# Moving the small parameter loads and the rows of x from SyncE's DMA queue to ScalarE's

## The chip, the cores and the metric

The kernel runs on one core of a Trainium2 chip. The metric is device time in microseconds (us) of one execution. A core has five engines that work in parallel, each on its own instructions in a fixed order: TensorE (PE in the profile; PEld is its weight load), VectorE (DVE), ScalarE (ACT), GpSimd (POOL) and SyncE (SP). Transfers are carried out by 16 DMA engines; an instruction on some engine's queue issues them. Here SP issues nearly all of them and does nothing else.

## What is computed

Two layers of a decoder trunk on x of 256 rows by 2048 columns, in float32. Each layer has a mixer and a feed-forward part; both are modulated by six vectors that a large matrix `w_ada` makes of one condition vector c. The opening of the kernel computes the first two of these vectors (`sh_m`, `sc_m`) for layer 0, the modulated input u and its projection:

```python
cond = silu(c)                                        # 1 x 2048
for l in range(2):
    mod = (cond @ w_ada[l] + b_ada[l]).reshape(B, 6, 1, 2048)    # w_ada[l]: 2048 x 12288
    sh_m, sc_m, gt_m, sh_f, sc_f, gt_f = [mod[:, i] for i in range(6)]
    u = x * (1 + sc_m) + sh_m
    proj = u @ w_in[l]                                # 2048 x 4896
    y_attn = sliding_window_attention(q, k, v of proj, attn_sinks[l], cos, sin)
    y_rwkv = rwkv7_group(rest of proj, rwkv_mu[l], w0, w2, a0, a2, g2, k_k, k_a, r_k, gn_w, gn_b, ...)
    mix = concatenate([y_attn, y_rwkv]) @ w_out[l]
    x = layer_norm(alpha * x + gt_m * mix, ln1_w[l], ln1_b[l])
    u = x * (1 + sc_f) + sh_f
    gate, up = split(u @ w_gate_up[l])
    x = layer_norm(alpha * x + gt_f * ((silu(gate) * up) @ w_down[l]), ln2_w[l], ln2_b[l])
```

## The kernel before

Each float32 operand of a matrix product is split into a rounded part `hi` and a rest `lo`, so that a product takes three TensorE matmuls: hi·hi, hi·lo and lo·hi. For a weight tile `raw` ScalarE makes `hi` by a cast (L380) and VectorE makes `lo` by a subtraction (L381); `steps` (L367 and following) does both and issues the load of `raw` (L372).

**The opening.** `parts` (from L1285) cuts the 16 blocks of 128 columns of x (k-tiles) into five groups of 4, 4, 2, 4 and 2. For each group it takes these steps:

- `ada_first` streams the columns of `w_ada` that belong to the group, in 16 tiles `ast` of 512 KB (L301). They lie in 8 buffers. VectorE multiplies each by its scalars of `cond` and adds it to the accumulator `aacc` (L304 for the first, L306 for the others).
- `ada_sums` transposes the accumulator on TensorE in blocks of 128 (tile `mb`, L277), ScalarE sums the rows of each block (L281), eight sums in a group of four k-tiles, and VectorE adds the bias `b_ada` and stores `mods` (L284), one instruction for every four sums.
- x comes in as the tile `xt` (L1300), two buffers in all. `make_u` transposes it (L354), ScalarE makes `uf` and its rounded form `u` from it with the `mods` (L358, L360), and VectorE makes the rest (L361).
- `tstream` multiplies `u` with the columns of `w_in` that the RWKV part needs first (L414 to L416).

Between the steps of the first group the generator `setup` is run for layer 0, and between those of the third group for layer 1. It loads all parameters that belong to a channel into a tile `prow` of 128 rows: `b_ada`, `ln1_w` and `ln1_b` (L175), ten others (L185), the last columns of `rwkv_mu` (L189) and, for layer 1, `rwkv_v0` (L193). Further it loads the attention sinks into `nsink` (L194). TensorE transposes `prow`, VectorE copies it to `par` (L200) and derives a few vectors `der` from it. `prow` has one buffer; the tile of layer 1 takes it when the one of layer 0 has been transposed. At the end of `parts`, `rope` loads the positions and makes tables of angles, and two DRAM tiles `tinv` are filled with zeros (L1313).

While this goes on, `ada_steps` streams the rest of `w_ada` in tiles of 128 x 1024 (L253, multiplied on L255 and L257); these go on far into the layer.

**What sets the order.** The program is written as generators, and a scheduler that estimates durations decides at build time in which order each engine gets its instructions. So an edit to one line can move instructions elsewhere. What a DMA must wait for is set then too. Eight semaphores, DMAHW0 to DMAHW7, are handed to the transfers in turn, in scheduled order, whatever the queue. A transfer is issued only when the one that had its semaphore before has landed, when its buffer is free and when its data exist; until then the issuing engine's queue stands, and with it all that follows on that engine.

The name `dma` in the code is `nc.sync.dma_start`, the queue of SP.

Of the kernel before, what the change touches and what calls it, by code (L numbers as in the profile page):

```python
# [19 lines left out]
P = 128  # L20
# [47 lines left out]
def hybrid_trunk_kernel(  # L68
# [7 lines left out]
    nc = tc.nc  # L76
    V, S, G, PE = nc.vector, nc.scalar, nc.gpsimd, nc.tensor
    dma = nc.sync.dma_start

    const = ctx.enter_context(tc.tile_pool(name="const", bufs=1))  # L80
    lhsp = ctx.enter_context(tc.tile_pool(name="lhsp", bufs=17))
# [69 lines left out]
    nsink = [const.tile([P, 16], F32, name=f"nsink{l}") for l in range(L)]  # L151
# [14 lines left out]
    def drv(l, nm, i, n=1):  # L166
        return der[l][:, DO[nm] + i:DO[nm] + i + n]

    def setup(sp, l):

        prow = sp.tile([P, 2, P], F32, tag="prow", bufs=1, name=f"prow{l}")
        G.memset(prow, 0.0)
        r = 0
        for nm, src, n in (("b_ada", b_ada[l], 96), ("ln1_w", ln1_w[l], 16), ("ln1_b", ln1_b[l], 16)):
            dma(prow[r:r + n, 0, :], src.rearrange("(r q) -> r q", q=P))  # L175
            PC[nm] = r
            r += n
            yield
        r = 0
        lst = [("ln2_w", ln2_w[l], 16), ("ln2_b", ln2_b[l], 16), ("w0", rwkv_w0[l], 8),  # L180
               ("a0", rwkv_a0[l], 8), ("k_k", rwkv_k_k[l], 8), ("k_a", rwkv_k_a[l], 8),
               ("r_k", rwkv_r_k[l].rearrange("h d -> (h d)"), 8), ("gn_w", rwkv_gn_w[l], 8),
               ("gn_b", rwkv_gn_b[l], 8), ("mu", rwkv_mu[l, 0:26 * P], 26)]
        for nm, src, n in lst:
            dma(prow[r:r + n, 1, :], src.rearrange("(r q) -> r q", q=P))  # L185
            PC[nm] = P + r
            r += n
            yield
        dma(prow[r:r + 1, 1, 0:32], rwkv_mu[l:l + 1, 26 * P:26 * P + 32])  # L189
        r += 1  # L190
        PC["v0"] = P + r
        if l > 0:
            dma(prow[r:r + 8, 1, :], rwkv_v0[l - 1].rearrange("(r q) -> r q", q=P))  # L193
        dma(nsink[l], attn_sinks[l:l + 1, :].to_broadcast([P, 16]))  # L194
        V.tensor_scalar_mul(nsink[l], nsink[l], -1.0)
        yield
        pt = bank()
        for i in range(2):
            PE.transpose(pt[:, i * P:(i + 1) * P], prow[:, i, :], ident)
        V.tensor_copy(par[l].rearrange("p a b -> p (a b)"), pt[:, 0:2 * P])  # L200
        V.tensor_scalar(drv(l, "omu", 0, 27), prm(l, "mu", 0, 27), -1.0, 1.0, ALU.mult, ALU.add)
        V.tensor_scalar_mul(drv(l, "w0h", 0, 8), prm(l, "w0", 0, 8), 0.5)
        V.tensor_scalar_mul(drv(l, "a0h", 0, 8), prm(l, "a0", 0, 8), 0.5)
        V.tensor_scalar_mul(drv(l, "kah", 0, 8), prm(l, "k_a", 0, 8), 0.5)
        V.tensor_scalar(drv(l, "okah", 0, 8), prm(l, "k_a", 0, 8), -0.5, 1.0, ALU.mult, ALU.add)
        V.tensor_scalar_mul(drv(l, "kkh", 0, 8), prm(l, "k_k", 0, 8), -0.5)
        V.tensor_scalar_mul(drv(l, "v0h", 0, 8), prm(l, "v0", 0, 8), 0.5)
# [1078 lines left out]
    with tc.tile_pool(name="pro", bufs=1) as pp:  # L1286
        xv = x[0].rearrange("(t p) d -> p t d", p=P)

        def parts():
            k0 = 0  # L1290
            for n in PARTS:
                o, w = k0 * P, n * P
                xt = pp.tile([P, 2, 512], F32, tag="xt", name="xt", bufs=2)[:, :, 0:w]
                side = setup(pp, 0) if k0 == 0 else setup(pp, 1) if k0 == 8 else iter(())
                rows = ada_first(pp, o, w)
                for j in range(512 // w, KT + 1, 512 // w):
                    next(rows)
                    next(side, None)
                    if j == 8:
                        dma(xt, xv[:, :, o:o + w])  # L1300
                for _ in side:
                    pass
                for _ in rows:
# [48 lines left out]
```

## Time and profile before

| quantity | value |
|---|---|
| time, median of 3 runs | 2694.9 us |
| lowest and highest of them | 2692.5 and 2695.86 us |
| time of the profiled execution | 2694.28 us |
| its span in the trace | 2692.6 us |
| TensorE busy | 2501.1 us, 93% of the span |
| VectorE, ScalarE, GpSimd busy | 1841.0, 1188.3 and 135.0 us |
| chain that ended last: TensorE, DMA, VectorE | 68%, 8%, 6% |
| moved by DMA | 637.49 MB, 237 GB/s on average |

The profile is of one execution. An engine is busy while it carries out an instruction; waiting and issuing DMAs don't count. The chain is followed back from the last instruction, at each step to what released it. In a timeline the bracket behind a row gives how long the engine had been idle before it, and what ended that wait; a row with x6 stands for six instructions in a row, and its duration is that of all of them.

### The profile page before, as it was taken

The numbers are of one execution on the slowest core, as the hardware profiler recorded it, in microseconds if no ns is written. First come the engines' busy times: TensorE is split into PE (matmuls) and PEld (weight loads), VectorE is DVE, ScalarE is ACT, GpSimd is POOL, SyncE is SP. The second block draws the span as 40 slices with busy tenths as digits, with TensorE's granted clock in tenths as the row PEclk, the third lists the DMA queues.
The fourth block names the chain that finished last, engine by engine and source line by source line (L and its number), as shares of the span: only waits on it lengthen the run. The fifth ranks groups of instructions, "written<-read, shape, count | busy, mean of one in ns | idle before, by whom it ended". The sixth has DMA issues, their size and how long they took to land.

```text
span 2692.6 us, 41752 instructions
## 1 busy us (share of the span) xinstructions
PE 2501.1 (93%) x15325; PEld 2093.1 (78%) x15325; DVE 1841.0 (68%) x2469; ACT 1188.3 (44%) x2029; POOL 135.0 (5%) x355
## 2 busy tenths in 40 slices
PE   3788998788999999999999999979899999999997
PEld 2687886567888888888889877867688888888887
DVE  6866767979877777777788677555764545545456
ACT  2364452435444444444445544534444444344442
POOL 1002112000000000000000022110000000000000
PEclk9789998899999999999999999989999999999999
DMA  9968668688998888889878586424756656666654
GB/s 315 381 188 253 198 191 238 180 317 296 353 330 309 297 303 312 293 295 308 308 263 304 174 259 188 117 72 144 253 172 188 190 186 196 195 189 189 193 188 149
DMA packets 351999, 637.49 MB, mean 237 GB/s; under 512 B 75894, under 2 KB 142898, under 8 KB 350258
## 3 DMA queue, kind: packets, MB, share of 16 engines
q1 hardware_dynamic: 351794, 634.82, 71.6%
q8 instruction: 120, 1.97, 0.3%
q14 instruction: 85, 0.70, 0.1%
HBM read 622.08 MB, written 12.62 MB: 236 GB/s over the span
## 4 chain that ended last, share of the span: by engine, by line
PE 68%; DMA 8%; DVE 6%; ACT 2%; issue 1%; POOL 1%; SPq 0%; DVEq 0%; POOLq 0%; ACTq 0%
PE acc L403 19%; PE acc L402 19%; PE acc L405 19%; DMA ast<-in_w_ada_dram 3%; DVE aacc L257 2%; PE acc L414 2%; PE acc L415 2%; PE acc L416 2%; DVE lo L381 1%; DMA raw<-in_w_gate_up_dram 1%; PE mb L1225 1%; DMA raw<-in_w_out_dram 1%; DMA yf<-yd 1%; PE mb L277 1%; ACT pr L947 0%
## 5 line engine op out<-in xcount | busy, mean ns | idle before, releaser
L380 ACT CAST hi<-raw 128x1024 fp32r<-128x1024 f32 (+2 forms) x728 | 758.5, 1044 | 1110.8 <-PE acc L405 833.1
L381 DVE TENSOR_TENSOR lo<-raw,hi 128x1024 fp32r<-128x1024 f32 (+2 forms) x728 | 880.2, 1212 | 519.8 <-PE acc L403 347.1
L403 PE MATMUL acc<-lo,u 128*128 128x512 f32 x1568 | 513.4, 395 | 11.9 <-DVE lo L381 11.8
L405 PE MATMUL acc<-hi,u 128*128 128x512 f32 x1568 | 505.8, 391 | 0.0
L257 DVE SCALAR_TENSOR_TENSOR aacc<-ast,cond,aacc 128x1024 f32<-128x1024 f32 x300 | 384.1, 1280 | 127.8 <-DMA ast<-in_w_ada_dram 126.6
L402 PE MATMUL acc<-hi,u 128*128 128x512 f32 x1568 | 457.2, 393 | 0.9 <-ACT u L360 0.5
L403 PEld LDWEIGHTS acc<-lo,u 128*128 128x128 f32 x1568 | 293.8, 189 | 76.4 <-DVE lo L381 16.2
L402 PEld LDWEIGHTS acc<-hi,u 128*128 128x128 f32 x1568 | 294.9, 188 | 63.4 <-ACT sg L1218 0.9
L405 PEld LDWEIGHTS acc<-hi,u 128*128 128x128 f32 x1568 | 295.2, 188 | 61.8 <-issue 0.5
L403 PE MATMUL acc<-lo,ht 128*128 128x512 f32 (+1 forms) x720 | 243.6, 377 | 3.0 <-DVE lo L381 2.9
L405 PE MATMUL acc<-hi,ht 128*128 128x512 f32 (+1 forms) x720 | 242.2, 375 | 0.0
L414 PE MATMUL acc<-u,hi 128*128 128x256 f32 x720 | 206.1, 293 | 14.0 <-ACT hi L380 14.0
L402 PE MATMUL acc<-hi,ht 128*128 128x512 f32 (+1 forms) x720 | 217.0, 376 | 0.0
L415 PE MATMUL acc<-u,hi 128*128 128x256 f32 x720 | 204.5, 291 | 0.0
L416 PE MATMUL acc<-u,lo 128*128 128x256 f32 x720 | 193.1, 294 | 7.1 <-DVE lo L381 7.1
L403 PEld LDWEIGHTS acc<-lo,ht 128*128 128x128 f32 x720 | 135.0, 188 | 29.3 <-DVE lo L381 5.6
L414 PEld LDWEIGHTS acc<-u,hi 128*128 128x128 f32 x720 | 141.9, 197 | 19.3 <-ACT hi L380 14.9
L405 PEld LDWEIGHTS acc<-hi,ht 128*128 128x128 f32 x720 | 135.6, 188 | 24.2
L402 PEld LDWEIGHTS acc<-hi,ht 128*128 128x128 f32 x720 | 134.8, 188 | 24.4
L415 PEld LDWEIGHTS acc<-u,hi 128*128 128x128 f32 x720 | 141.7, 197 | 2.6 <-issue 1.6
L416 PEld LDWEIGHTS acc<-u,lo 128*128 128x128 f32 x720 | 133.8, 197 | 11.6 <-DVE lo L381 9.0
L1067 POOL TENSOR_TENSOR brs<-brs,mhalf 128x1 f32<-128x1 f32 x8 | 7.6, 955 | 1698.7 <-DVE brs L1066 772.1
(349 smaller groups left out, 2901.1 us busy)
## 6 DMA issues: line engine op xcount, KB each, us to landing
ast<-in_w_ada_dram SPq DMA_DIRECT2D x368, 512.0 KB
raw<-in_w_gate_up_dram SPq DMA_DIRECT2D x704, 256.0 KB
raw<-in_w_down_dram SPq DMA_DIRECT2D x176, 512.0 KB
raw<-in_w_in_dram SPq DMA_DIRECT2D x82, 512.0 KB
raw<-in_w_out_dram SPq DMA_DIRECT2D x64, 512.0 KB
raw<-in_w_in_dram SPq DMA_DIRECT2D x120, 256.0 KB
ast<-in_w_ada_dram SPq DMA_DIRECT2D x32, 256.0 KB
lnw<-in_ln_w_dram SPq DMA_DIRECT2D x4, 1024.0 KB
```

The lines of the kernel that those rows point to most:

```text
L257: ins = V.scalar_tensor_tensor(acc, t, cond[:, j:j + 1], acc, ALU.mult, ALU.add)
L277: PE.transpose(b[:, i * P:(i + 1) * P], blocks[q + i], ident)
L380: S.copy(h, fl)
L381: ins = V.tensor_tensor(r, fl, h.bitcast(F32), ALU.subtract)
L402: PE.matmul(bt, lhsT=xh, rhs=hi[:, c0:c0 + w], start=st, stop=False)
L403: PE.matmul(bt, lhsT=xh, rhs=lo[:, c0:c0 + w], start=False, stop=False)
L405: PE.matmul(banks[t][q][:, 0:w], lhsT=xl, rhs=hi[:, c0:c0 + w], start=False, stop=sp_)
L414: PE.matmul(bt, lhsT=hi[:, c0:c0 + w], rhs=xh, start=st and opens, stop=False)
L415: PE.matmul(bt, lhsT=hi[:, c0:c0 + w], rhs=xl, start=False, stop=False)
L416: PE.matmul(bt, lhsT=lo[:, c0:c0 + w], rhs=xh, start=False, stop=sp_ and closes)
L1067: G.tensor_tensor(rs[:, 0:1], rs[:, 0:1], mhalf[:, 0:1], ALU.pow)
L1225: PE.transpose(b[:, i * T + t * P:i * T + (t + 1) * P], hh[t][:, (2 * k2 + i) * P:(2 * k2 + i + 1) * P], ident)
```

## The change

A second name for issuing transfers is made, `side_dma`, which is the queue of ScalarE. The loads of `setup` (parameters into `prow`, and `nsink`) and the load of `xt` in `parts` use it. All others, the weights among them, remain on SP's queue. 36 issues move: 29 of parameters, 2 of `nsink`, 5 of `xt`. Lines after L77 have a number that is higher by one in the changed kernel.

```diff
@@ -76,6 +76,7 @@
     dma = nc.sync.dma_start
+    side_dma = nc.scalar.dma_start
@@ -172,7 +173,7 @@
         for nm, src, n in (("b_ada", b_ada[l], 96), ("ln1_w", ln1_w[l], 16), ("ln1_b", ln1_b[l], 16)):
-            dma(prow[r:r + n, 0, :], src.rearrange("(r q) -> r q", q=P))
+            side_dma(prow[r:r + n, 0, :], src.rearrange("(r q) -> r q", q=P))
@@ -182,16 +183,16 @@
         for nm, src, n in lst:
-            dma(prow[r:r + n, 1, :], src.rearrange("(r q) -> r q", q=P))
+            side_dma(prow[r:r + n, 1, :], src.rearrange("(r q) -> r q", q=P))
...
-        dma(prow[r:r + 1, 1, 0:32], rwkv_mu[l:l + 1, 26 * P:26 * P + 32])
+        side_dma(prow[r:r + 1, 1, 0:32], rwkv_mu[l:l + 1, 26 * P:26 * P + 32])
...
-            dma(prow[r:r + 8, 1, :], rwkv_v0[l - 1].rearrange("(r q) -> r q", q=P))
-        dma(nsink[l], attn_sinks[l:l + 1, :].to_broadcast([P, 16]))
+            side_dma(prow[r:r + 8, 1, :], rwkv_v0[l - 1].rearrange("(r q) -> r q", q=P))
+        side_dma(nsink[l], attn_sinks[l:l + 1, :].to_broadcast([P, 16]))
@@ -1297,7 +1298,7 @@
                     if j == 8:
-                        dma(xt, xv[:, :, o:o + w])
+                        side_dma(xt, xv[:, :, o:o + w])
```

The scheduler answers with other orders. Three places matter in what follows. In the rows, a line is followed by the operation and by what it writes and reads; the number behind a tile's name tells one tile from another, x6 is six in a row.

*SP, from the start of the program.* `ast` are weight tiles of `w_ada`, `prow_170` is the parameter tile of layer 0, `raw` are weight tiles of `w_in`. Before:

```order
L154 DMA crow<-in_c_dram 16x128
L301 DMA ast<-in_w_ada_dram 128x2x512 x6
L175 DMA prow_170<-in_b_ada_dram 96x128
L175 DMA prow_170<-in_ln_w_dram 16x128
L175 DMA prow_170<-in_ln_b_dram 16x128
L185 DMA prow_170<-in_ln_w_dram 16x128
L185 DMA prow_170<-in_ln_b_dram 16x128
L185 DMA prow_170<-in_rwkv_w_dram 8x128
L301 DMA ast<-in_w_ada_dram 128x2x512
L185 DMA prow_170<-in_rwkv_a_dram 8x128
L301 DMA ast<-in_w_ada_dram 128x2x512
L185 DMA prow_170<-in_rwkv_k_k_dram 8x128
```

And now:

```order
L155 DMA crow<-in_c_dram 16x128
L302 DMA ast<-in_w_ada_dram 128x2x512 x10
L373 DMA raw<-in_w_in_dram 128x2x256
L302 DMA ast<-in_w_ada_dram 128x2x512
L373 DMA raw<-in_w_in_dram 128x2x128
L302 DMA ast<-in_w_ada_dram 128x2x512
L373 DMA raw<-in_w_in_dram 128x2x256
L302 DMA ast<-in_w_ada_dram 128x2x512
L373 DMA raw<-in_w_in_dram 128x2x128
L302 DMA ast<-in_w_ada_dram 128x2x512 x2
L373 DMA raw<-in_w_in_dram 128x3x288
```

The parameters of layer 0 stood behind the sixth `ast` and between the later ones; now ten `ast` stand in a row, and then only weights follow.

*ScalarE, from the start of the program.* L281 are the row sums of the first group, L380 the casts of raw tiles, L358 and L360 make `u`. Before:

```order
L155 ACT_TABLE_LOAD
L155 ACTIVATE crow<-crow 16x128
L380 CAST hi<-raw 128x768 x2
L281 ACTIVATE mb,asum<-mb 128x128 x2
L380 CAST hi<-raw 128x864
L281 ACTIVATE mb,asum<-mb 128x128 x6
L358 ACTIVATE uf<-mb,mods_135 128x256
L360 ACTIVATE u<-mb,mods_135 128x256
L358 ACTIVATE uf<-mb,mods_135 128x256
```

And now, from the loads of layer 1's parameters (`prow_843`) on, with the semaphores that each waits for (those named DMAHW are the eight of the transfers; L282 is the old L281); ahead of these rows stand two loads of `xt`, two of `nsink`, the 14 of `prow_170`, the first casts and five loads of `prow_843`:

```order
L186 DMA prow_843<-in_rwkv_k_k_dram 8x128 [waits DMAHW0_49]
L186 DMA prow_843<-in_rwkv_k_a_dram 8x128 [waits DMAHW1_49]
L186 DMA prow_843<-in_rwkv_r_k_dram 8x128 [waits DMAHW2_49]
L186 DMA prow_843<-in_rwkv_gn_w_dram 8x128 [waits DMAHW4_49]
L186 DMA prow_843<-in_rwkv_gn_b_dram 8x128 [waits DMAHW5_49]
L282 ACTIVATE mb,asum<-mb 128x128 [waits DVE_49,PE_49]
L186 DMA prow_843<-in_rwkv_mu_dram 26x128 [waits DMAHW6_49]
L282 ACTIVATE mb,asum<-mb 128x128 [waits Activation_49]
L190 DMA prow_843<-in_rwkv_mu_dram 1x32 [waits DMAHW0_49]
L282 ACTIVATE mb,asum<-mb 128x128 [waits Activation_49]
L194 DMA prow_843<-in_rwkv_v_dram 8x128 [waits DMAHW1_49]
L282 ACTIVATE mb,asum<-mb 128x128 [waits Activation_49]
```

Loads for layer 1, which stood on SP and in the third group, now stand ahead of and between the first four row sums of the first group. `DMAHW6`, for which the load of `mu` waits (L186, 26x128), was last given to the seventh `ast` of the second group; `DMAHW0` in the first row was last given to a raw tile of the second group. The last two loads wait for loads of `prow_843` itself, those of the first two rows.

*VectorE, from the last multiply-add of the first group on.* `mods_135` are the modulation vectors of layer 0; L361, L381 and L306 are as described, and L224 to L241 belong to the tables of angles. Before:

```order
L306 SCALAR_TENSOR_TENSOR aacc<-ast,cond,aacc 128x1024
L381 TENSOR_TENSOR lo<-raw,hi 128x768 x2
L284 SCALAR_TENSOR_TENSOR mods_135<-asum,par_131 128x4
L304 TENSOR_SCALAR aacc<-ast,cond 128x1024
L284 SCALAR_TENSOR_TENSOR mods_135<-asum,par_131 128x4
L306 SCALAR_TENSOR_TENSOR aacc<-ast,cond,aacc 128x1024
L195 TENSOR_SCALAR nsink_138<-nsink_138 128x16
L221 CAST posf<-posi 128x2
L361 TENSOR_TENSOR u<-uf,u 128x256
```

And now (numbers higher by one), the rows around the two instructions that store `mods`:

```order
L242 TENSOR_SCALAR ang<-ang 128x64
L240 TENSOR_TENSOR rc<-rc,wrap 128x64
L307 SCALAR_TENSOR_TENSOR aacc<-ast,cond,aacc 128x1024
L242 TENSOR_SCALAR rc<-rc 128x64
L285 SCALAR_TENSOR_TENSOR mods_135<-asum,par_131 128x4
L256 TENSOR_SCALAR aacc<-ast,cond 128x1024
L285 SCALAR_TENSOR_TENSOR mods_135<-asum,par_131 128x4
L307 SCALAR_TENSOR_TENSOR aacc<-ast,cond,aacc 128x1024
L362 TENSOR_TENSOR u<-uf,u 128x256 x2
L307 SCALAR_TENSOR_TENSOR aacc<-ast,cond,aacc 128x1024 x2
L362 TENSOR_TENSOR u<-uf,u 128x256
```

The tables of angles, which came behind the `mods`, come ahead of them now; the two `mods` stand some sixteen rows further back, and 14 of the 16 multiplies of the second group stand behind the first of them.

## Rows read from the trace of the kernel before

**Rows 1.** The page: its first line and the busy time of each engine.
```profile
span 2692.6 us, 41752 instructions
...
PE 2501.1 (93%) x15325; PEld 2093.1 (78%) x15325; DVE 1841.0 (68%) x2469; ACT 1188.3 (44%) x2029; POOL 135.0 (5%) x355
```

**Rows 2.** Stretches: us, busy PE, PEld, DVE, ACT, POOL (count), PEclk, DMA share, GB/s.
```profile
0.00:20.00 20.00, 0.70 (x2) 0.36 (x2) 11.07 (x20) 1.59 (x2) 9.47 (x62) 1.00 0.81 262
20.00:40.00 20.00, 2.65 (x9) 1.61 (x9) 13.86 (x21) 5.32 (x19) 0.31 (x1) 1.00 1.03 358
40.00:60.00 20.00, 17.36 (x113) 16.19 (x114) 17.12 (x31) 6.80 (x13) 0.00 (x0) 1.00 0.93 305
...
80.00:140.00 60.00, 43.31 (x286) 40.10 (x286) 51.26 (x72) 23.46 (x63) 0.00 (x0) 0.83 1.07 380
...
0.00:2.50 2.50, 0.00 (x0) 0.00 (x0) 1.02 (x11) 1.44 (x2) 1.75 (x11) 1.00 0.12 13
```

**Rows 3.** Timeline of ACT from 32 us: start, us, engine, line, operation, idle before.
```profile
33.03 0.83 ACT L380 CAST hi<-raw 128x768 fp32r<-128x768 f32 x1 [30.38 <-DMA raw<-in_w_in_dram]
...
34.92 0.26 ACT L281 ACTIVATE mb<-mb 128x128 f32<-128x128 f32 x1
...
41.20 0.56 ACT L358 ACTIVATE uf<-mb,mods 128x256 f32<-128x256 f32 x1 [1.21 <-PE mb L354]
```

**Rows 4.** Timeline of DVE, the first group's multiplies.
```profile
5.48 0.89 DVE L304 TENSOR_SCALAR aacc<-ast,cond 128x1024 f32<-128x1024 f32 x1 [2.22 <-DMA ast<-in_w_ada_dram]
...
22.05 8.17 DVE L306 SCALAR_TENSOR_TENSOR aacc<-ast,cond,aacc 128x1024 f32<-128x1024 f32 x6 [2.85 <-DMA ast<-in_w_ada_dram]
```

**Rows 5.** Timeline of SP: its first weight tiles and parameters.
```profile
1.25 3.27 SPq L301 DMA_DIRECT2D ast<-in_w_ada_dram  x6
4.83 0.33 SPq L175 DMA_DIRECT2D prow<-in_b_ada_dram  x1
...
10.74 0.40 SPq L301 DMA_DIRECT2D ast<-in_w_ada_dram  x1
```

**Rows 6.** Waits of SP, 0 to 330 us: us in total, times, longest us.
```profile
SPq L185 <- DMA ast<-in_w_ada_dram: 8.3, 9, 1.5
```

**Rows 7.** Timeline of DVE, 37 to 80 us.
```profile
37.20 0.16 DVE L284 SCALAR_TENSOR_TENSOR mods<-asum,par 128x4 f32<-128x4 f32 x1 [1.33 <-ACT mb L281]
...
40.03 0.17 DVE L284 SCALAR_TENSOR_TENSOR mods<-asum,par 128x4 f32<-128x4 f32 x1 [2.01 <-ACT mb L281]
...
48.68 1.05 DVE L381 TENSOR_TENSOR lo<-raw,hi 128x864 fp32r<-128x864 f32 x1
...
49.75 0.42 DVE L361 TENSOR_TENSOR u<-uf,u 128x256 fp32r<-128x256 f32 x1
...
63.83 1.28 DVE L306 SCALAR_TENSOR_TENSOR aacc<-ast,cond,aacc 128x1024 f32<-128x1024 f32 x1 [2.19 <-DMA ast<-in_w_ada_dram]
...
71.30 1.22 DVE L381 TENSOR_TENSOR lo<-raw,hi 128x1024 fp32r<-128x1024 f32 x1 [1.03 <-ACT hi L380]
...
76.39 1.28 DVE L306 SCALAR_TENSOR_TENSOR aacc<-ast,cond,aacc 128x1024 f32<-128x1024 f32 x1
...
79.07 0.46 DVE L381 TENSOR_TENSOR lo<-raw,hi 128x288 fp32r<-128x288 f32 x1
```

**Rows 8.** Timeline of ACT, the end of the opening.
```profile
171.05 0.47 ACT L454 ACTIVATE xwa<-lb,der 128x256 f32<-128x256 f32 x1 [3.11 <-PE lb L416]
```

**Rows 9.** Waits of DVE, 80 to 140 us: us in total, times, longest us.
```profile
DVE mods L284 <- ACT mb L281: 2.6, 3, 1.1
...
DVE u L361 <- ACT u L360: 1.5, 3, 0.6
...
DVE lo L381 <- DMA ast<-in_w_ada_dram: 0.4, 1, 0.4
DVE aacc L306 <- DMA ast<-in_w_ada_dram: 0.4, 1, 0.4
```

**Rows 10.** The chain that ended last, 400 to 460 us: start, us, what.
```profile
412.53 5.83 DMA ast<-in_w_ada_dram
```

## The prediction

> **What bounds the kernel now.** I read the page first, then the opening of the kernel engine by engine, because that is where the edited lines run. TensorE is busy for 2501.1 of 2692.6 us [rows 1]; after the first 170 us the kernel is a stream of matmuls that hardly stops, and only a late start or a wait on the chain to TensorE can be won or lost there. The profiled execution took 2694.28 us, 0.6 us under the median of 2694.9, so that sums made in its trace stand as they are for the time.
>
> The opening is another matter. TensorE has done 0.70 us of work by 20 us and 2.65 us more by 40 us, while the DMA engines move 262, 358 and 305 GB/s in the first three stretches and 380 GB/s in 80 to 140 us [rows 2]. It is bound by the weights of w_ada. SyncE (its queue is SP) issues them as tiles `ast` of 512 KB; VectorE multiplies each into an accumulator (L306, 1.28 us a tile); after 16 tiles come transposes, eight row sums on ScalarE (L281) and the two `mods` (L284), and only then can ScalarE and VectorE make `u` (L358 to L361), which the first matmuls need. In the trace `u` starts at 41.20 [rows 3]. VectorE waits for `ast` more than once on the way, 2.85 us in one place [rows 4].
>
> Part of the low rate is SP's doing. SP issues six `ast` by 4.5 us, then a run of small parameter loads stands in the same queue, and its seventh `ast` goes out at 10.74 [rows 5]. Each such load also waits for the transfer that had its semaphore before it: nine waits of L185 cost SP 8.3 us [rows 6]. The eight DMA semaphores are handed round to the issues in the order of the program, whatever the queue, and an issue waits until the transfer eight turns earlier (on its semaphore) has landed.
>
> **What the change gives SP.** 36 issues leave SP's queue: 29 of parameters, 2 of `nsink`, 5 of x. One costs SP 0.33 us [rows 5] plus its wait. The most that this can give is the DMA rate of the steady stretch from the beginning: (380−262)·20 + (380−358)·20 + (380−305)·20 = 4300, divided by 380 is 11.3 us; the first 2.5 us carry 13 GB/s [rows 2] because nothing has landed yet, and no queue cures that, so 2.5·(380−13)/380 = 2.4 us come off: 8.9 us at most. The least is 0, if the later limits hide it.
>
> **What it adds to ScalarE.** In time of its own, 36 issues at 0.33 us are 12 us, in a stretch where ScalarE is busy for 1.59 + 5.32 + 6.80 of 60 us [rows 2]. Up to the first cast it waits 30.38 us for a raw tile [rows 3], and that idle time hides the first 18 issues and their own waits; without that cover they would cost 18·0.33 = 5.9 us. I count nothing for them.
>
> The waits of the next 15 are what I count. The order shown ahead puts the loads of *layer 1* (`prow_843`) in ScalarE's queue ahead of, and between, the first four row sums of the first group. A wait on one of their semaphores is a wait for what SP has put on it: that of `mu` is the seventh `ast` of the *second* group, and behind it are three of those four sums, all of the second four, and `u`. Before, nothing stood there, and the sums ran from 34.92, right behind the casts [rows 3].
>
> When does that tile land? Counting in SP's order what goes out up to it, in units of 512 KB: 16 + 7 `ast`, 2 tiles of x, 1344 KB of raw tiles of the first group, two of 260 KB (L1313), 2 `ast` of the mixer's own w_ada stream, 2 raw tiles of the second group and about 0.3 MB of small ones, together 33.3 units or 17.45 MB. The first unit lands at about 5.48, where the first multiply starts [rows 4]. At 380 GB/s one takes 0.5243/380 = 1.38 us, so the last is there at 5.48 + 32.3·1.38 = 50.0. That is an estimate, and it already contains the whole gain of the denser stream. `mods` came 37.20 − 34.92 = 2.3 us after the first sum and the second one 2.8 us later, at 40.03 [rows 3, 7]. So now: sums at 50, first `mods` at about 52.5, second at 55.5, `u` 1.2 us behind it (40.03 to 41.20) at 56.7 instead of 41.20: **15.5 us late**.
>
> Not all of that reaches the end, since VectorE has work in store. In the new order the first `mods` (L285 now) stands ahead of 14 of the second group's multiply-adds; VectorE runs dry near 38 and stands until 52.5. What is left for it up to the end of the second group is 14·1.28 + 4·0.42 (`u`) + 1.05 + 4·1.22 + 0.46 (`lo`) = 26.0 us [rows 7], and I put 3 us of waits on ScalarE and TensorE on top (from the single waits of 1.03 and 2.19 us among those rows). From 55.5 that ends at 84.5; before it ended at 76.39 + 1.28 = 77.7 [rows 7]. The late start has become 6.8 us.
>
> Is it made up by 171 us, where the opening ends with `xwa` on L454 [rows 8]? In 80 to 140 us VectorE is busy for 51.26 of 60 us [rows 2], and of its waits there those on w_ada's own tile before a multiply-add are 0.4 us, once; with a second such wait before a `lo`, 0.8 us may be regained [rows 9]. The larger ones, 2.6 us on row sums and 1.5 on `u`, belong to the chain itself [rows 9]. So **6 us** reach the end of the opening.
>
> Bounds of this term: it is 0 if nothing waits on TensorE or ScalarE and the semaphores come free at the earliest (26.0 us of work, sums released near 45 us, 5 us earlier: 50.5 + 26.0 is 76.5, before's 77.7). It is about +12 if the DMA engines keep to the mean of the first three stretches, 308 GB/s, for which the same 17.45 MB end at 5.48 + 32.3·1.70 = 60: sums 10 us later, of which VectorE's waits for `ast` then hide some half.
>
> On the rate a page speaks too. The trace of before has one queue with data, and shows the DMA engines at 380 GB/s from it when nothing holds it [rows 2]. The Trainium skill, "DMA: Bandwidth & Descriptors", section "Issuing engines are not separate DMA queues", says that transfers started by different engines run on the same 16 DMA engines and interleave, and that starting them on several saves only the sequencers' time to start them, usually a small one. By that rule the change would give back the issue time alone, which speaks against the gain and for the second rival below. The 8.3 us of waits in SP's row [rows 6] are more than issue time, so the row goes beyond the rule.
>
> **What moves beyond the opening.** The scheduler has reordered other stretches as well: VectorE's order is unchanged from about 200 to 400 us, then differs by some ten to forty places in the attention of layer 0 and around the mixer of layer 1, and in the last 690 us nothing moves. The multiset of instructions is the same. I know no sign for this. A single DMA wait on the chain costs 5.83 us there [rows 10]; one more or one fewer is my bound, ±5.8 us, and I take 0.
>
> **Sum.** 2694.3 + 6 + 0 = 2700 us. With the ends 0 and +12 and ±5.8 beside it: 2688 to 2712, the outer ends not both at once.
>
> **Rivals.**
> *Faster, by the denser stream.* All 8.9 us of the rate arrive: 2694.3 − 8.9 = 2685. For it: VectorE waits 2.85 us for an `ast` [rows 4] and SP does stand on semaphores of its own small loads [rows 6]. Against it: three of the first four sums wait for a tile of the second group. It decides at about 45 us: with the first group's sums released before that, VectorE isn't out of work long and the denser stream carries; after that the wait on ScalarE does.
> *No change.* SP's lateness was no more than its waits for transfers that the DMA engines were busy with anyway, and VectorE's store of work takes up the late sums: 2694. For it: VectorE works 42 of the first 60 us [rows 2] and needs 1.28 us per tile, hardly less than the 1.38 us that one takes to land.
> *The whole delay.* `u` is 15.5 us late and TensorE passes all of it on: 2710. Against it: VectorE, not TensorE, sets the pace of 80 to 140 us [rows 2].
>
> **Chances.** Forecast 0.55, faster rival 0.19, no change 0.19, the whole delay 0.07. A measurement of this kernel can tell about 0.2%, 5.4 us. Of the forecast's 0.55 I put 0.40 beyond +5.4 us and 0.15 within it. Faster by over 0.2%: 0.19. Within: 0.15 + 0.19 = 0.34. Slower: 0.40 + 0.07 = 0.47. The range runs from 2687, which takes in the forecast's lower end and nearly the faster rival, to 2711, which takes in the whole delay.
>
> **What would show it.** In the trace of after: six or more `ast` issued without a stop and over 340 GB/s in 0 to 20 us (the denser stream); ScalarE's waits for an `ast` or raw tile between its first sums, which end near 50; VectorE idle from about 38 to 52 ahead of the first `mods`; the last multiply-add of the second group near 84.5; `xwa` near 177 instead of 171. The prediction is wrong at its main step if the sums end before 45, wrong in what follows if they end at 50 and `xwa` is on time, and wrong in the reorder term if `xwa` is at 177 and the end isn't 6 us late.

## The result and the profile after

The changed kernel takes 2699.54 us (median of 18 runs, 2693.66 to 2706.76) against 2694.68 us of the kernel before (18 runs, 2687.27 to 2701.37): ratio 1.0021, 95% interval 1.0011 to 1.003. It is slower by about 5 us; the interval is clear of 1, and its middle lies at the 0.2% that I had set as a limit. The forecast was 2700. The profiled execution took 2702.37 us, 2.8 us above its median; that of before lay 0.4 us under its own, so the two traces differ by 8 us where the medians differ by 5.

The page of the changed kernel: its first line, the busy times and the two queues that now carry data (q10 is new).

```profile
span 2700.6 us, 41744 instructions
...
PE 2501.8 (93%) x15325; PEld 2093.4 (78%) x15325; DVE 1839.3 (68%) x2469; ACT 1188.1 (44%) x2029; POOL 128.6 (5%) x355
...
q1 hardware_dynamic: 349344, 632.46, 70.9%
q10 hardware_dynamic: 2450, 2.37, 0.3%
```

The engines are as busy as before [rows 1]: no work was added, it came later. By stretches, columns as in [rows 2]:

```profile
0.00:20.00 20.00, 0.70 (x2) 0.36 (x2) 10.76 (x22) 1.59 (x2) 7.08 (x62) 1.00 0.91 308
20.00:40.00 20.00, 1.56 (x5) 0.90 (x5) 15.22 (x26) 1.66 (x2) 0.31 (x1) 1.00 0.97 327
40.00:60.00 20.00, 2.23 (x8) 1.44 (x8) 4.70 (x13) 4.46 (x20) 0.00 (x0) 1.00 0.97 343
60.00:80.00 20.00, 18.13 (x132) 17.27 (x132) 17.38 (x18) 8.44 (x14) 0.00 (x0) 1.00 0.84 285
80.00:140.00 60.00, 45.84 (x311) 43.45 (x312) 55.11 (x73) 22.40 (x57) 0.00 (x0) 0.83 1.07 379
```

The stream is denser at first (308 GB/s instead of 262 in 0 to 20 us), as SP's timeline explains: ten tiles in a row, where six had stood [rows 5].

```profile
1.25 15.67 SPq L302 DMA_DIRECT2D ast<-in_w_ada_dram  x10
```

But in 40 to 60 us TensorE works for 2.23 us instead of 17.36 and VectorE for 4.70 instead of 17.12 [rows 2]. ScalarE's timeline shows why (ACTq rows are the DMAs that it issues; time and duration, then what it is):

```profile
29.48 0.83 ACT L381 CAST hi<-raw 128x768 fp32r<-128x768 f32 x1 [4.29 <-DMA raw<-in_w_in_dram]
40.28 0.32 ACTq L176 DMA_DIRECT2D prow<-in_b_ada_dram  x1
...
48.78 0.32 ACTq L186 DMA_DIRECT2D prow<-in_ln_b_dram  x1
49.14 0.91 ACT L381 CAST hi<-raw 128x864 fp32r<-128x864 f32 x1 [18.83 <-DMA prow<-in_ln_b_dram]
...
53.31 0.31 ACTq L186 DMA_DIRECT2D prow<-in_rwkv_gn_b_dram  x1
53.73 0.26 ACT L282 ACTIVATE mb<-mb 128x128 f32<-128x128 f32 x1 [3.67 <-DMA prow<-in_rwkv_k_k_dram]
...
54.10 0.31 ACTq L186 DMA_DIRECT2D prow<-in_rwkv_mu_dram  x1
54.47 0.26 ACT L282 ACTIVATE mb<-mb 128x128 f32<-128x128 f32 x1 [0.37 <-ACT mb L282]
...
59.67 0.56 ACT L359 ACTIVATE uf<-mb,mods 128x256 f32<-128x256 f32 x1 [1.21 <-PE mb L355]
```

Between the second cast at 29.48 and the third at 49.14 ScalarE does nothing but stand at loads of layer 1's parameters: the first of them goes out at 40.28, the fifth at 48.78, the twelfth at 53.31. The cast between them is put down to one of these loads, 18.83 us. The first row sum runs at 53.73 where it had run at 34.92 [rows 3], and `u` starts at 59.67 instead of 41.20. (Seven of these loads, not five, stand ahead of the rows of ScalarE's order shown with the change, so that twelve precede the first sum.)

What each load waited for, the semaphore updates in the trace tell. The first was released at 40.11 by a small load `w2a` that SP had issued at 33.20; the third, fourth and fifth at 44.56, 46.07 and 48.76 by tiles of w_ada that SP had issued at 37.04, 37.79 and 39.85; the eighth at 51.49 by a raw tile issued at 43.07. Apart from loads of their own group they all waited for SP's transfers, as the prediction has it. VectorE stands with ScalarE:

```profile
8.00 1.01 DVE L305 TENSOR_SCALAR aacc<-ast,cond 128x1024 f32<-128x1024 f32 x1 [3.69 <-DMA ast<-in_w_ada_dram]
...
55.67 0.16 DVE L285 SCALAR_TENSOR_TENSOR mods<-asum,par 128x4 f32<-128x4 f32 x1 [12.61 <-ACT mb L282]
...
58.50 0.16 DVE L285 SCALAR_TENSOR_TENSOR mods<-asum,par 128x4 f32<-128x4 f32 x1 [2.00 <-ACT mb L282]
...
85.04 1.28 DVE L307 SCALAR_TENSOR_TENSOR aacc<-ast,cond,aacc 128x1024 f32<-128x1024 f32 x1
```

Idle for 12.61 us ahead of the first `mods`; the second follows at 58.50. The second group's last multiply-add ends at 85.04 + 1.28 = 86.3, against 77.7 [rows 7].

VectorE's standing comes back to the weights: an `ast` needs a buffer that a multiply-add has freed. SP's waits for multiply-adds, 40 to 80 us (us in total, times, longest), before and in the changed kernel, and before's stretch of 60 to 80 us:

```profile
SPq L301 <- DVE aacc L306: 0.2, 1, 0.2
```
```profile
SPq L302 <- DVE aacc L307: 10.5, 9, 2.9
```
```profile
60.00:80.00 20.00, 10.07 (x69) 9.63 (x67) 14.34 (x14) 3.85 (x7) 0.00 (x0) 0.74 1.05 378
```

In 60 to 80 us the changed kernel moves 285 GB/s where before moved 378. By the rates of the stretches it had moved 1.1 MB more than before by 60 us, and 0.8 MB less by 80.

Where the lead and the lag go afterwards, the two executions of `xwa` tell, one at the end of each layer's first projection (line L454, L455 in the changed kernel; the two times are the first and the last start). Before, and once more before (`before_again` below):

```profile
L454 ACT ACTIVATE xwa<-lb,der x2: 474/474/474, 171.1 to 1455.3; 128x256 f32<-128x256 f32 x2
```
```profile
L454 ACT ACTIVATE xwa<-lb,der x2: 474/474/474, 169.0 to 1459.0; 128x256 f32<-128x256 f32 x2
```

The changed kernel, and the same once more (`after_again`):

```profile
L455 ACT ACTIVATE xwa<-lb,der x2: 474/474/474, 175.2 to 1467.8; 128x256 f32<-128x256 f32 x2
```
```profile
L455 ACT ACTIVATE xwa<-lb,der x2: 474/474/474, 173.8 to 1465.9; 128x256 f32<-128x256 f32 x2
```

The opening ends 175.2 and 173.8 instead of 171.1 and 169.0: 4.5 us later in the mean. At the start of layer 1 the lag is 9.7 us in the mean, and at the end of the span 8.0 and 3.1 us (2700.6 and 2697.6 against 2692.6 and 2694.5), 5.6 in the mean.

### The profile page after: what moved, and what is told of

Its sections match the earlier page's. It is cut to its first block, busy times and chain, and to the rows that moved or that the text cites. A ratio compares the mean times of both kernels' runs of the same rounds, so it can differ in the third digit from the quotient of the medians.

```text
span 2700.6 us, 41744 instructions
## 1 busy us (share of the span) xinstructions
PE 2501.8 (93%) x15325; PEld 2093.4 (78%) x15325; DVE 1839.3 (68%) x2469; ACT 1188.1 (44%) x2029; POOL 128.6 (5%) x355
## 4 chain that ended last, share of the span: by engine, by line
PE 66%; DMA 8%; DVE 7%; issue 1%; ACT 1%; POOL 1%; SPq 0%; DVEq 0%; POOLq 0%; ACTq 0%
PE acc L404 19%; PE acc L403 18%; PE acc L406 18%; DMA ast<-in_w_ada_dram 3%; DVE aacc L258 2%; DVE lo L382 2%; PE acc L417 1%; PE acc L416 1%; PE acc L415 1%; DMA raw<-in_w_gate_up_dram 1%; DMA yf<-yd 1%; PE mb L1226 1%; DMA qkv<-stg 0%; POOL ttl L736 0%; DMA raw<-in_w_out_dram 0%
## 5 line engine op out<-in xcount | busy, mean ns | idle before, releaser
L381 ACT CAST hi<-raw 128x1024 fp32r<-128x1024 f32 (+2 forms) x728 | 758.3, 1044 | 1117.8 <-PE acc L406 815.4
```

What stands on the lines that cost most here:

```text
L381: S.copy(h, fl)
```

## Experiments

The theory: ScalarE executes in order, a load on its queue stands until its semaphore's last transfer has landed, and the loads of layer 1, which the scheduler put ahead of the first row sums, hold these. The rivals: (A) a second queue takes from the rate at which the weights land; (B) the order that the scheduler made behind the opening sets the difference. In the table, "sum" is the first row sum of the first group, "first" the first multiply on w_ada, `xwa` the end of the opening, "rest" the span less `xwa`, all of the profiled execution in us; ratio and interval are those of all runs against the kernel before on the same chip. The medians are of several chips, so that only the ratios can be compared down the table. A profiled execution can lie several us off its kernel's median: `only_x` 7.7, `setup_pool_x_sp` 7.3, `five` 8.5 and `l1_pool` 3.8 under it, `setup_act_x_sp` 4.1, `late_l1` 3.1 and the changed kernel 2.8 above it, the others within 1.

| kernel | layer 0's / layer 1's loads, x | first | sum | xwa | rest | median | ratio (95%) |
|---|---|---|---|---|---|---|---|
| before | SP / SP, SP | 5.5 | 34.9 | 171.1 | 2521.5 | 2694.7 | |
| before_again | the same | 5.2 | 35.0 | 169.0 | 2525.5 | one run | |
| changed | ACT / ACT, ACT | 8.0 | 53.7 | 175.2 | 2525.4 | 2699.5 | 1.0021 (1.0011 to 1.003) |
| after_again | the same | 7.4 | 53.1 | 173.8 | 2523.8 | one run | |
| l1_sp | ACT / SP, ACT | 7.6 | 39.1 | 170.2 | 2522.8 | 2695.7 | 0.9997 (0.9984 to 1.0009) |
| only_l1 | SP / ACT, SP | 6.5 | 51.9 | 174.6 | 2523.8 | 2700.4 | 1.002 (1.0004 to 1.0037) |
| only_l0 | ACT / SP, SP | 6.2 | 34.3 | 164.8 | 2524.5 | 2691.7 | 0.9987 (0.9973 to 1.0) |
| only_x | SP / SP, ACT | 8.1 | 40.4 | 164.7 | 2523.7 | 2697.9 | 1.0008 (0.9995 to 1.0022) |
| late_l1 | ACT / ACT late, ACT | 7.8 | 38.6 | 173.9 | 2535.1 | 2707.6 | 1.0045 (1.0031 to 1.0058) |
| l1_pool | ACT / GpSimd, ACT | 7.2 | 40.7 | 164.1 | 2524.3 | 2694.0 | 0.9987 (0.9976 to 0.9999) |
| l1_pool_x_sp | ACT / GpSimd, SP | 6.4 | 34.1 | 161.3 | 2523.9 | 2687.9 | 0.9971 (0.9958 to 0.9983) |
| setup_pool_x_sp | GpSimd / GpSimd, SP | 5.3 | 44.8 | 161.5 | 2521.3 | 2692.0 | 0.9985 (0.9975 to 0.9996) |
| setup_act_x_sp | ACT / ACT, SP | 9.2 | 53.8 | 180.5 | 2524.6 | 2702.8 | 1.0024 (1.0011 to 1.0036) |
| five | ACT / 5 ACT and 10 GpSimd, ACT | 8.2 | 49.6 | 172.4 | 2524.1 | 2706.7 | 1.0026 (1.0011 to 1.0042) |

All edits but `late_l1` and `five` are of one kind, a choice of queue by layer, and another for x:

```diff
     def setup(sp, l):
-
+        side_dma = (nc.scalar.dma_start, nc.sync.dma_start)[l]
...
-                        side_dma(xt, xv[:, :, o:o + w])
+                        nc.scalar.dma_start(xt, xv[:, :, o:o + w])
```

This is `l1_sp`. The others put `nc.sync`, `nc.scalar` or `nc.gpsimd` into the three places as the table's second column says.

**One part undone: layer 1 back on SP (`l1_sp`).**

> Undoes one part of the change: the 15 loads of layer 1's parameters and its nsink go back to SyncE's queue; layer 0's parameters and x stay on ScalarE's. Theory (ScalarE's row sums are held by the semaphores of layer 1's loads): the first row sum runs near 35 us instead of 53.7, u near 42 instead of 59.7, the last multiply-add of the second group ends at or before 77.7 and xwa near 169 to 171; time 2688 to 2696. Rival A (two queues share the DMA engines and the weights land later): the sums run after 45 us and the time stays at 2697 to 2702. Rival B (the time comes from the order the scheduler made after the opening): xwa moves as the theory says, but the time stays at 2697 or more, with the difference after 400 us.

The sum is back at 39.1, `mods` at 40.73 and 43.56, `xwa` at 170.2 and the time at that of before. ScalarE's first sum now waits for the transposes and for no load:

```profile
39.14 0.26 ACT L282 ACTIVATE mb<-mb 128x128 f32<-128x128 f32 x1 [3.43 <-PE mb L278]
```

The theory holds at ScalarE. The sum came 4 us later than I had put it, and the second group's last multiply-add ends at 80.4 instead of 77.7 or before; x goes out first here too (below). As the source of the 19 us rival A falls: layer 0's loads and x are still on the second queue, and the sums are not held.

**One part alone: layer 1 on ScalarE (`only_l1`).**

> Does one part alone: only layer 1's parameters and its nsink go on ScalarE's queue; layer 0's parameters and x stay on SyncE's as before. Theory: the sums of the first group are held as in the changed kernel, first mods at 50 us or later, xwa 4 us late or more (175 or later), time 2697 to 2706. Rival A: with only 16 small loads on the second queue little is shared, sums near 37 us, time 2694. Rival B: xwa near 171 and any time from 2688 to 2701.

As the theory has it, `mods` at 55.09, 1.0020 as the whole change; only `xwa`, 174.6, is 0.4 us short of what I gave:

```profile
47.88 0.32 ACTq L186 DMA_DIRECT2D prow<-in_ln_w_dram  x1
48.24 0.83 ACT L381 CAST hi<-raw 128x768 fp32r<-128x768 f32 x1 [45.38 <-DMA ast<-in_w_ada_dram]
...
51.86 0.26 ACT L282 ACTIVATE mb<-mb 128x128 f32<-128x128 f32 x1
```

Here already the first cast stands for 45.38 us (30.38 in [rows 3]) behind four loads of layer 1, put down to an `ast` of SP's. These 15 loads of about 0.3 us of issue each, with one of `nsink`, alone cost as much as the whole change.

**The other part: layer 0 alone (`only_l0`), x alone (`only_x`).**

> Does the other part alone: layer 0's parameters and its nsink go on ScalarE's queue; layer 1's parameters and x stay on SyncE's. Theory: ScalarE issues them while it would wait anyway, nothing holds the sums, SyncE issues eight weight tiles in a row: first multiply at 5.5 us, sums a few us earlier than before's 34.92 (30 to 34), xwa at 165 to 170, time 2686 to 2694. Rival A: sums at or after 37 us, time 2695 or more. Rival B: xwa as the theory says, the time anywhere from 2685 to 2700.

> Only the five loads of x go on ScalarE's queue. Theory: the two first tiles of x (512 KB each) are issued at once and share the DMA engines with the first weight tiles, so the first multiply starts near 8 us as in the changed kernel instead of 5.48; the sums are not held and run at 35 to 37; xwa within 2 us of 171; time 2692 to 2698. Rival A: the shared engines cost more, sums after 40 us. Rival B: xwa at 171 and the time anywhere from 2688 to 2701.

With layer 0 alone SP issues eight tiles in a row and the first stretch is as dense as in the changed kernel, while nothing is held:

```profile
0.00:20.00 20.00, 0.70 (x2) 0.36 (x2) 11.83 (x22) 1.59 (x2) 7.63 (x62) 1.00 0.90 307
...
40.00:60.00 20.00, 17.52 (x120) 17.02 (x121) 16.29 (x26) 6.63 (x13) 0.00 (x0) 1.00 0.88 295
```

TensorE works for 17.52 us in 40 to 60 as before, and `xwa` comes 6.3 us earlier than in [rows 8]. But the first multiply, 6.2, and the sum, 34.3, are later than I had put them, and the second group ends at 78.3 against before's 77.7: the gain of this kernel is made behind the second group. The time, 0.9987, agrees but its interval just reaches 1.

With x alone the first multiply starts at 8.1, 2.6 us later than in [rows 4], as expected: two tiles of x of 512 KB go out with the first weights. The sum is at 40.4, 5.5 us later than before and just past the 40 that I had named as a sign of rival A; so for large transfers ahead of the weights that rival holds. `xwa` is at 164.7, 4 us earlier than I said. Its profiled execution is the fastest of its 12 runs, so this `xwa` is not that of the median, 2697.9; whether moving x alone gains or costs stays open within 0.9995 to 1.0022. Two pairs further down the table that differ in x alone, `l1_sp` and `only_l0` (0.9997 and 0.9987) and `l1_pool` and `l1_pool_x_sp` (0.9987 and 0.9971), have the kernel with x on ScalarE behind, though the intervals overlap.

**The place instead of the queue (`late_l1`).** A multiplication by a `mods` value of the second group is put between the zeroing of layer 1's `prow` and its loads:

```diff
         G.memset(prow, 0.0)
+        if l: G.tensor_scalar_mul(prow, prow, mods[0][:, 4:5])
```

> All 36 loads on ScalarE's queue as in the changed kernel, but layer 1's parameter tile is multiplied on GpSimd by a modulation value of the second group before it is loaded (its zeros stay zeros), so that its 15 loads stand in ScalarE's queue behind the second group's eight row sums instead of ahead of and between the first group's. Theory (a load on ScalarE's queue waits for its semaphore and holds what stands behind it): the first sums run at 39 to 41 us as with layer 1 on SyncE's queue, and ScalarE stands for 8 to 15 us between 85 and 110 us instead, between the third group's work; whether it costs the end depends on the slack there: xwa between 170 and 178. Rival (not the place but the number of transfers on ScalarE's queue costs): first sums after 45 us. Second rival (the waits are short because SyncE runs less far ahead there): no single wait over 2 us and xwa at 170, time 2693 to 2696.

The first sum is free again, 38.6, although all 36 loads are on ScalarE, so their number is not what holds (the edit also adds an instruction on GpSimd, 1.28 us at 76.28); and the standing has moved to where the loads are now:

```profile
84.73 0.32 ACTq L177 DMA_DIRECT2D prow<-in_ln_b_dram  x1
85.15 0.56 ACT L360 ACTIVATE uf<-mb,mods 128x256 f32<-128x256 f32 x1 [6.88 <-DMA raw<-in_w_in_dram]
...
92.19 0.56 ACT L360 ACTIVATE uf<-mb,mods 128x256 f32<-128x256 f32 x1 [4.26 <-DMA prow<-in_ln_b_dram]
```

6.88 and 4.26 us ahead of two `uf`, both behind loads. `xwa` is at 173.9 and, with 1.0045 from five runs, this is the slowest kernel of all. Of that the opening shows only 2.8 us; its rest is 10 us longer than any other's. That part is lost behind the opening, where rival B, the order, is the likely source; I haven't traced it.

**Another engine with nothing to do (`l1_pool`, `l1_pool_x_sp`, `setup_pool_x_sp`).**

> The changed kernel with layer 1's 15 parameter loads and its nsink on GpSimd's queue, which has nothing else to do there; layer 0's and x stay on ScalarE's. They are issued early, and keep semaphores of their own. Theory: no row sum waits for them: first sum at 37 to 41 us, xwa at 166 to 171, time 2688 to 2696. Rival A (a further queue takes from the weights): sums after 45 us, time 2697 or more.

GpSimd issues the 15 loads in 10.4 us, each for 0.5 us, with waits of its own that hold nobody; the ninth waits for the first, since GpSimd's loads go round among eight semaphores of their own (its timeline):

```profile
28.18 0.58 POOL L176 DMA_DIRECT2D prow<-in_b_ada_dram  x1 [0.31 <-POOL prow L173]
...
33.51 0.51 POOL L186 DMA_DIRECT2D prow<-in_rwkv_k_a_dram  x1 [1.30 <-DMA prow<-in_b_ada_dram]
...
38.07 0.51 POOL L194 DMA_DIRECT2D prow<-in_rwkv_v_dram  x1
```

Sum at 40.7, `xwa` at 164.1 (2 us earlier than I gave), time 0.9987 (0.9976 to 0.9999). Against the changed kernel the edit differs only in the engine of 16 small loads (the scheduler's orders follow from it), and the opening is 11 us shorter. A third queue beside the other two does no harm, which speaks against rival A for small loads once more.

> Layer 0's parameters on ScalarE's queue, layer 1's on GpSimd's, x on SyncE's. Theory: first multiply at 6 us (x is not ahead of the first weight tiles), sums at 33 to 35 us, second group without small loads between its weight tiles, xwa at 163 to 166; time 2684 to 2692, the best so far. Rival B (order after the opening decides): xwa as expected and a time anywhere up to 2697.

With x on SP behind the first eight weight tiles the first multiply is at 6.4, the sum at 34.1, `xwa` at 161.3:

```profile
161.32 0.47 ACT L455 ACTIVATE xwa<-lb,der 128x256 f32<-128x256 f32 x1 [3.12 <-PE lb L417]
```

The time is 2687.9, ratio 0.9971 (0.9958 to 0.9983): the one version that beats both kernels clearly, by 0.29%, 7.8 us, against before.

> All parameters of both layers on GpSimd's queue, x on SyncE's, nothing on ScalarE's. Theory: as the kernel with layer 0 on ScalarE and layer 1 on GpSimd, within 3 us: first multiply at 6 us, sums at 33 to 36 us, xwa at 163 to 167, time 2684 to 2693. If issuing costs GpSimd more than the 0.33 us that SyncE needed, layer 0's parameters come late and with them the transposes of prow: mods would then wait for par, which the trace shows.

Here the transposes for the sums are put down to `par` of layer 0, the sign that I had named for late loads (TensorE's timeline, and VectorE's):

```profile
43.66 1.11 PE L278 MATMUL mb<-ident,aacc 128*128 128x128 f32 x4 [17.39 <-DVE par L201]
```
```profile
41.32 1.28 DVE L307 SCALAR_TENSOR_TENSOR aacc<-ast,cond,aacc 128x1024 f32<-128x1024 f32 x1 [1.85 <-DMA ast<-in_w_ada_dram]
...
43.18 0.42 DVE L201 COPY par<-mb 128x256 f32<-128x256 f32 x1
```

But GpSimd's loads are not the cause. The last of layer 0's is out at 20.84 and TensorE has transposed `prow` by 26.3; VectorE copies it to `par` only at 43.18, as this copy stands in VectorE's order behind the first group's last multiply-add, which ends at 42.6. The likely reason is SP's new order: six raw tiles go out ahead of the group's twelfth `ast`, where before all went out behind the sixteenth. So the sums come at 44.8, 9 us later than I expected, and `xwa` is at 161.5 all the same. This lateness is work done in another order, and no hold: ahead of its two `mods` VectorE is idle for 0.33 and 2.67 us, where the changed kernel has 12.61 and 2.00. The time, 0.9985, is nearer 1 than that of `l1_pool_x_sp`, and this profile is the fastest of its kernel's runs, so that a small cost isn't ruled out.

**Is the gain of layer 0 added to the hold or swallowed by it (`setup_act_x_sp`)?**

> The parameters of both layers on ScalarE's queue, x on SyncE's. With layer 0's parameters alone there the opening ended 6.3 us before that of the kernel before, with layer 1's alone 3.5 us behind it. Theory (the hold swallows the gain): the sums wait for layer 1's loads all the same, the first multiply at about 6 us, the first sum at 47 to 53, xwa at 172 to 176, time 2697 to 2702. Rival (the two effects add up): sums held but xwa at 168 or before, time 2691 to 2695.

Swallowed, and more than that: the first multiply is at 9.2 instead of the 6 I gave, the sum at 53.8, and `xwa` at 180.5, later than I said. Now already the second cast of the first group stands behind loads (17.37 us; in the changed kernel it is the third), and with it VectorE's `lo`; how much of the 180.5 is this isn't settled. The time is 2702.8, just above my 2702 (ratio 1.0024, 1.0011 to 1.0036).

```profile
47.83 0.32 ACTq L176 DMA_DIRECT2D prow<-in_ln_b_dram  x1
48.24 0.83 ACT L381 CAST hi<-raw 128x768 fp32r<-128x768 f32 x1 [17.37 <-DMA ast<-in_w_ada_dram]
```

**A smaller dose (`five`).** Of layer 1's loads only those of 96 and 16 rows stay on ScalarE:

```diff
-            side_dma(prow[r:r + n, 1, :], src.rearrange("(r q) -> r q", q=P))
+            (nc.gpsimd.dma_start if l and n != 16 else nc.scalar.dma_start)(prow[r:r + n, 1, :], src.rearrange("(r q) -> r q", q=P))
```

(and `nc.gpsimd` for the 1x32 piece of `mu`, `v0` and `nsink` of layer 1).

> The changed kernel with five of layer 1's loads (b_ada, ln1_w, ln1_b, ln2_w, ln2_b) on ScalarE's queue ahead of the first sums, the ten others and its nsink on GpSimd's. Theory (each load ahead of the sums waits for a transfer of SyncE's that lands later than the last): the first sum lies between that without such loads (40.7) and that with 15 of them (53.7): 44 to 49; since VectorE's store of work hides a delay up to about 45, xwa lies at 164 to 170 and the time at 2692 to 2697. Rival (any such load holds the sums fully): first sum after 51, xwa at 174 or later, time 2698 or more.

```profile
48.38 0.32 ACTq L186 DMA_DIRECT2D prow<-in_ln_b_dram  x1
...
49.56 0.26 ACT L282 ACTIVATE mb<-mb 128x128 f32<-128x128 f32 x1
```

The sum, 49.6, follows the fifth load by 1.2 us. It lies between the two ends (40.7 and 53.7), though 0.6 us above the range that I gave, so neither "any load holds fully" nor "a load costs its 0.3 us". But `xwa`, 172.4, is 2 us later than the theory had it, and the time, 2706.7, is what the rival had said (2698 or more): by the times of all runs five loads cost as much as fifteen. Eight of its ten runs lie 6 to 11 us above the profiled one (2698.25), whose rest is like all others'; what those runs lose isn't in any trace I have, and it stays open.

**What one execution can tell (`after_again`, `before_again`).**

> The changed kernel once more, to tell what of the difference behind the opening belongs to the order and what to one execution. If the order makes it: first sum 53.7, xwa 175.2 and the mixer of layer 1 (its xwa) at 1467 to 1468 again. If it is one execution's: xwa of the opening within 0.5 us, and that of layer 1 anywhere between 1459 and 1469.

> The kernel before once more, for the same question. If executions of one order agree: first sum 34.9, xwa 171.0, that of layer 1 at 1455 to 1456. If not: the opening the same within 0.5 us and layer 1's xwa up to 5 us off.

Events inside the opening agree within 0.6 us up to the sums and within 2.0 at `xwa`; at the start of layer 1 within 3.7. So neither guess was quite right: the opening spreads more, and the 12.5 us of the first pair at layer 1 were partly one execution's. What repeats is the order's own waits between 475 and 715 us. TensorE, waits in that stretch, us in total, times, longest, in both executions of the changed kernel:

```profile
PE m L750 <- ACT yt L865: 4.0, 1, 4.0
...
PE m L757 <- DVE yx L753: 2.5, 1, 2.5
```
```profile
PE m L750 <- ACT yt L865: 4.0, 1, 4.0
PE m L757 <- DVE yx L753: 2.5, 1, 2.5
```

The first is new against before, the second was 1.0 us in its first execution. Others became shorter, and by the end the lag is that of the opening again.

## Why the prediction came out right, step by step

**The range, the side and the size were right**: 2700 forecast, 2699.5 measured, +6 against +4.9 us. The range, 2687 to 2711, took in every rival but the faster one, so that it alone proves little; the side and the held sums say more. The steps were less even than the sum.

*The denser stream.* Over 340 GB/s in 0 to 20 us was wanted, 308 came. The term was too large for the first stretch, and x going out first is not the reason: `only_l0`, with x behind eight weight tiles, has 307. It was also not kept: the lead of 1.1 MB at 60 us had become a lag of 0.8 MB at 80, as VectorE, while it stood, freed no buffers. At 80 to 140 us the rate is 379 GB/s as before [rows 2].

What x does is delay the first tile: the kernels with x on ScalarE start the first multiply at 7.2 to 8.2 us. Of the others, those with nothing on that queue at the start have 5.2 to 5.5, those with one load of `nsink` there 6.2 to 6.5, and `setup_act_x_sp`, with two such loads, 9.2; why the second costs so much I can't say. I had counted two tiles of x in the sum of bytes but let the first weight tile land at before's 5.48.

The Trainium skill, "DMA: Bandwidth & Descriptors", section "Issuing engines are not separate DMA queues", says that transfers of several engines interleave on the same 16 DMA engines. The unchanged 379 GB/s and the late first tile agree with it. The Trainium skill says in the same section that issuing from several engines saves only the sequencers' issue time. `only_l0` moves 15 issues, 5 us at 0.33 each [rows 5], and its opening is 4.2 to 6.3 us shorter than the two of before; that is of the same size, but no run here parts the issue time from the waits of [rows 6], which left SP's queue with it.

*The hold.* The main step was right, and the runs show it: `l1_sp` takes it away, `only_l1` has it alone, `l1_pool` keeps all else of the edit. Its place in the queue was named too far back, though. I named `mu` as the load that decides; `mu` went out at 54.10, between two sums 0.74 us apart, and cost 0.37 us. The 12 loads ahead of the first sum had already done the holding, as the first of them could only go at 40.28. So that the sums came near the forecast is in part luck: the last waits that held the first sum ended at 51.49 (a raw tile) and at 52.98 (a load of the group itself), and not with the tile that I had counted to. That tile, the seventh `ast` of the second group, was put at 50.0 and landed at 54.08; of the 4.1 us the first tile, 2.5 us later than in before, is the likely larger part.

*`mods` and `u`.* 52.5, 55.5 and 56.7 forecast, 55.67, 58.50 and 59.67 measured: the same 3 us late throughout, so the steps between them, taken from [rows 3, 7], were right to 0.2 us; from the first sum to the first `mods` it took 1.9 us where I had 2.3.

*VectorE's store of work.* Dry near 38 and back at 52.5 forecast; it ran dry at 43.0 (its last instruction before the 12.61 us) and came back at 55.67. The end of the second group: 84.5 forecast, 86.3 measured; 27.8 us from the second `mods` where I had 29.0.

*What is regained by 171 us.* This term was mis-sized. I gave 0.8 us back; the lag fell from 86.3 − 77.7 = 8.6 to 4.1 us. I had looked for the gain in VectorE's waits on w_ada's tiles [rows 9]. In the changed kernel VectorE is busy for 55.11 us in 80 to 140 us instead of 51.26 [rows 2], but so it is in kernels that hold nothing, `only_l0` and `l1_pool`:

```profile
80.00:140.00 60.00, 45.57 (x308) 41.73 (x309) 55.03 (x79) 26.32 (x67) 0.00 (x0) 0.83 1.06 379
```
```profile
80.00:140.00 60.00, 45.47 (x309) 42.10 (x309) 54.60 (x77) 25.92 (x63) 0.00 (x0) 0.82 1.01 362
```

From the end of the second group to `xwa` the two executions of before take 93.4 and 92.9 us, those of the changed kernel 88.9 and 87.2, `l1_pool`, whose second group ends early at 75.9, 88.2, and `only_l0`, on time at 78.3, 86.5. So this stretch became shorter with the new orders, whether a kernel comes late or not, and lateness is not what shortens it; only `late_l1` takes longer, 100.4. What in the orders makes it shorter isn't shown. The second group's end, 1.8 us later than forecast, and this error of −3.7 us partly cancel, which is why `xwa`, 175.2 where I had 177, looks better than its terms: that part is luck.

*The reorder.* ±5.8 us, taken as 0. The rest behind the opening is 2521 to 2526 us in 13 of the 14 profiled executions, whatever the order; the kernel before alone gave 2521.5 and 2525.5. So 0 was right here, and the bound too. `late_l1`, with 2535, shows that an order can cost twice as much.

*The rivals.* Faster by 8.9 us: the gain exists, −7 to −10 us at `xwa` against [rows 8], but in kernels that hold nothing; in the times of all runs it is 0.13% (`l1_pool`) to 0.29% (`l1_pool_x_sp`), 3.5 to 7.8 us. The point from which it decides was put at 45 us. With x and layer 0 on ScalarE in all three, sums at 40.7, 49.6 and 53.7 go with `xwa` at 164.1, 172.4 and 175.2, so that one us of hold costs 0.7 to 0.9 us; before's mean of 170 lies at about 47. These are single executions, in which `xwa` varies by 2 us, and the times of all runs put `five` beside the changed kernel, so the slope is rough. 47 is near my 45, yet not for my reason: little of the hold is absorbed by VectorE's store, it is set against two gains. One is SP's, which no longer carries layer 1's loads: `l1_pool` is ahead of `l1_sp` by 6.1 us at `xwa` (0.9987 and 0.9997 in time). The other is the shorter stretch behind the second group. In `setup_pool_x_sp` the sums are 10 us late and `xwa` isn't, but there VectorE doesn't stand ahead of `mods`; in `five` it does, for 10.71 us. The whole delay, 2710, and no change, 2694, didn't happen, though part of the 95% interval lies within 0.2% of before.

## What to carry to other kernels

A DMA issued from an engine that also computes is an instruction in that engine's order: before moving it there, count what it must wait for (a semaphore shared with the weight stream above all) and who stands behind it. Loads that nobody needs soon are the dangerous ones, since a scheduler that sees an idle engine pulls them forward, ahead of work that is needed; give them to an engine without work in that stretch, as GpSimd here. And look at the gain and the loss of such an edit apart, by moving one group of transfers at a time: here a gain of 7 us in the opening (`l1_pool`) and a loss of 11 (from there to the changed kernel) were hidden in one lag of 4; in the times of all runs, a gain of 0.13% and a loss of 0.34% in one +0.21%.

## What the runs showed that I hadn't expected

The first tiles on a second queue are not free: with 512 KB of x issued there at 0.8 us, the first multiply on w_ada starts at 7.2 to 8.2 us instead of 5.2 (`only_x` against the two of before: 8.1 against 5.5 and 5.2). One and the same order gives `xwa` 1.4 to 2.0 us apart and times over a range of 13 to 14 us within 18 runs, so that a single profile can be several us off its median; differences of 5 us needed the runs, and the profiles only for the place. A load issued by GpSimd occupied it for 0.5 us, one on SP or ScalarE its queue for 0.3.
